# Weight-block sums of a Strassen up projection: made by transfers inside DRAM during attention, or by GpSimd during the MLP

## The chip, the cores and the metric

The kernel runs on one core of one Trainium2 chip. The metric is the device time of one execution in microseconds. A core has five engines that work beside one another: PE (TensorE, the matmuls; PEld are its weight loads), DVE (VectorE), ACT (ScalarE), POOL (GpSimd) and SP (SyncE, which only issues transfers here). Transfers are carried by 16 DMA engines of the core; SP, ACT and POOL can issue them.

## The reference

A two-layer encoder over two sequences (512 and 256 tokens, width 1024) that share the weights. Layer 0 mixes 2-D neighbourhood attention and grouped-query attention (GQA), layer 1 is differential attention. After each attention comes a squared-ReLU MLP of width 4096:

```python
for layer in range(DEPTH):
    ...                                   # attention of the layer, residual add
    h = rmsnorm(x, ln_mlp[layer])
    x = x + jnp.square(jax.nn.relu(h @ w_up[layer])) @ w_down[layer]
return rmsnorm(x, ln_f)
```

All arrays are float32.

## The kernel before

**Staging.** All 768 tokens are held together. The program is four stages in a row: `even_attention` (layer 0), `mlp(0)`, `odd_attention` (layer 1), `mlp(1)`. Activations and weights are split into a high and a low part (`wsplit`, L80 on ACT for the high part, L81 on DVE for the low part), and every product is three matmuls (high-high, high-low, low-high).

**The up projection.** `h @ w_up` is done by Strassen's method in Winograd's form: seven products in place of eight, on 2 x 2 blocks. The columns of `w_up` are walked in 16 steps (`mp`, 0 to 15) of 256 columns; each step has four weight blocks a11, a22, a12, a21 of 128 x 512 values. Steps 0 and 1 use the plain blocks with eight products (while the sums of activations are made by `second()`), steps 2 to 15 use the seven products, 84 matmuls each. The seven need four sums of weight blocks, s1 = a21 + a22, s2 = s1 + a11, s3 = a11 + a21, s4 = a12 + s2 (signs are in the layout). Products are called by number: 1 needs a11, 2 a12, 3 s4, 4 a22, 5 s1, 6 s2, 7 s3. PE runs them in the order 1, 3, 2, 6, 4, 7, 5. In `weights()` the blocks are loaded by two transfers of 512 KB into `wraw` tiles (3 buffers), POOL makes the four sums (L843) into `s` tiles, and the splits are written in the order (1,4), (6,5), (7,3), (2). High and low parts have 4 buffers each (`whilo`).

**The norm in it.** The MLP's RMSNorm is applied late: `nm.rstd()` (L161 to L166) sums squares by matmul, `ms` is made by DVE (L164) and the power -1/2, `rt`, by POOL (L166); `nm.spread` (L178, `pb`) spreads it over partitions by PE. This happens while steps 2 and 3 run. `finish(z)` writes the squared activations to DRAM tiles `T`, from ACT's queue (L879) and POOL's (L887), and the down projection reads them back (`tr`).

**The attentions.** `attention(units, chain, targets)` weaves 48 attention units (softmax of one token tile of one head or pair) into a chain of projection steps; `targets` says up to which step of the chain each unit comes. Weights of the projections are loaded by SP, group by group, through the same 3 `wraw` buffers (`wload`, L74). POOL does small things there: the powers `rn` of the q/k norms (L356, L357), the scaling of one GQA softmax map (L502), parts of the rotary embedding (L677, L678) and the powers of layer 1's sub-norm (L724).

**What sets the order.** The order of the instructions on an engine is not that of the text. A planner takes the program as written and places instructions one by one, each as soon as its engine, its data and its buffers are free by the planner's own estimates of the costs; among those that are ready the one written earlier goes first. On the chip each engine then keeps that order strictly, and an instruction that waits holds up all that stand behind it on its engine.

Of the kernel before, what the change touches and what calls it, by code (L numbers as in the profile page):

```python
# [37 lines left out]
def kernel(ctx: ExitStack, tc: tile.TileContext, a: dict, y: bass.AP):  # L38
# [37 lines left out]
    def wsplit(hi, lo, raw, dve=False):  # L76
        if dve:
            nc.vector.tensor_copy(hi, raw)
        else:
            nc.scalar.activation(hi, raw, AF.Copy)  # L80
        nc.vector.tensor_tensor(out=lo, in0=raw, in1=hi.bitcast(F32), op=ALU.subtract)  # L81
# [151 lines left out]
                fn()  # L233
            self.due = []

    def attention(units, chain, targets):

        live = []
        n = len(targets) - 1
        for i in range(n):  # L240
            a, b = targets[i], targets[i + 1]
            chain.pull(a)
            live.append(units[i]())
            live[-1][0]()
# [56 lines left out]
    def even_attention():  # L301
# [306 lines left out]
                       lambda: out_proj("w_out_e", o, lambda m: a["xT"][:, m, :], x, 0)])  # L608
        units = [G(gqa_unit, j, t) for j in range(4) for t in range(TT)]
        units += [G(na_unit, p, t) for p in range(4) for t in range(TT)]  # L610
        attention(units, chain, ramp((52, 72, 88, 104, 120, 140, 172, 196, 232)))
        chain.drain()
        return o, x, es

# [1 line left out]
    def odd_attention(xs, nm, sg, spill):  # L616
# [121 lines left out]
            order += [G(proj_v, h // 2)] * (h % 2 == 0) + [G(proj_qk, h)]  # L738
        chain = Chain(order + [lambda: out_proj("w_out_o", o, lambda m: spill[:, m, :], x, 0)])
        units = [G(diff_unit, h, t) for h in range(8) for t in range(TT)]  # L740
        attention(units, chain, ramp((56, 92, 128, 164, 200, 236, 272, 306, 336)))
        chain.drain()
        return o, x, es

# [24 lines left out]
    def mlp(layer, src, o, x, es):  # L769
# [47 lines left out]
        g2 = g2s.enter_context(tc.tile_pool(name="g2", bufs=4, side="right", reuse_waits="tile"))  # L817
        up = g2s.enter_context(tc.tile_pool(name="up", bufs=3, side="right", reuse_waits="tile"))

        def weights(plain=False):  # L820


            raws = []
            for _ in range(2):
                raw, loads = wload("w_up", 1024)
                loads[0]()
                raws.append(raw)
            a11, a22, a12, a21 = (r[:, i * 512 : (i + 1) * 512] for r in raws for i in range(2))
            if plain:
                out = {}  # L830
                for t, ij in zip(raws, (((0, 0), (1, 1)), ((0, 1), (1, 0)))):
                    hi, lo = whilo(1024)
                    wsplit(hi, lo, t)
# [5 lines left out]
            out = {}  # L839
            for ps_, t in (((1, 4), raws[0]), ((6, 5), sa), ((7, 3), sb), ((2,), raws[1])):  # L840
                if t is sa:
                    for d_, x_, y_ in ((s1, a21, a22), (s2, s1, a11), (s3, a11, a21), (s4, a12, s2)):
                        nc.gpsimd.tensor_tensor(out=d_, in0=x_, in1=y_, op=ALU.add)  # L843
# [49 lines left out]
        ws = [weights(True) for _ in range(2)]  # L893
        for w in ws:
            z = ztile()
            pss = [bank(n) for n in (1, 6, 2, 4)]
# [17 lines left out]
            return th  # L914

        for mp in range(2, FF // 256):
            w = weights()
# [322 lines left out]
```

## Time and profile before

| what | value |
|---|---|
| time, median of 3 runs | 1790.25 us (1785.74 to 1792.01) |
| the profiled execution | 1793.21 us, span 1791.2 us, mean granted TensorE clock 0.982 |
| PE, PEld busy | 96%, 92% of the span |
| DVE, ACT, POOL busy | 77%, 46%, 33% |
| moved by transfers | 235.42 MB, mean 131 GB/s |
| layer 0's attention units on PE | 59.7 to 349.6 us |
| layer 0's up products | about 372 to 634 us |
| layer 1's attention units on PE | 924 to 1247 us |
| layer 1's up products | about 1272 to 1534 us |

How to read the rows. Times are microseconds from the start of the span; a mean of one instruction is in nanoseconds. A group's row is: line, engine, operation, out<-in, shapes, count | busy us, mean ns | idle time of the engine just before, and what ended most of it. In a table by stretches each engine has its busy time and the number of its instructions; the last three columns are the granted clock, the mean busy share of the 16 DMA engines and the GB/s. A row "A L1 <- B L2: x, n, y" says that A's instructions of L1 waited for B's of L2, x us in all, n times, y at most. In a timeline, the first two numbers are start and duration, and brackets hold the idle time before and what ended it; neighbours of one kind are merged. In the queues' rows stand packets, MB and the share of 16 engines' span that the packets took; an issue's row ends with KB each and the median time from issue to landing. q1 are SP's transfers, q10 ACT's, q0 POOL's. "SPq" and the like are an engine's issuing side.

### The profile page before, as it was taken

To read this page: it belongs to the slowest core of one execution; us is meant where nothing else is said; L and a number is where in the kernel's file an instruction comes from. 1 tells how busy PE (TensorE), PEld (TensorE's weight loads), DVE (VectorE), ACT (ScalarE), POOL (GpSimd) and SP (SyncE) were. 2 spreads that over 40 slices of the span, in tenths; PEclk is the share of its full clock that TensorE was granted. 3 is DMA by queue.
4 is the path that set the end of the run, shared out by engine and by line. 5 is a ranking of instruction groups with operands and counts; after the bars stand their busy time and mean duration, and the time that the engine had idled before them with its cause. 6 is when DMAs were issued, how large, how long until landed. Compare 5 with 4: busy or idle time off the path is not lost.

```text
span 1791.2 us, 28400 instructions
## 1 busy us (share of the span) xinstructions
PE 1728.0 (96%) x10994; PEld 1644.2 (92%) x10994; DVE 1385.5 (77%) x2182; ACT 827.2 (46%) x1509; POOL 583.7 (33%) x456
## 2 busy tenths in 40 slices
PE   7999999998999999999999999999988999999997
PEld 7887888898999989999999999988988999899997
DVE  7777746597888867799656767776878888787995
ACT  6665544363333444444435555554633334444441
POOL 2321000023555404475021212220225554053750
PEclk8999999999999999999999999999999999999998
DMA  5111223312554587664311101112125545977621
GB/s 173 41 33 37 68 71 104 121 48 72 189 163 164 182 329 294 245 204 158 97 46 48 48 25 45 54 57 95 48 69 180 166 166 170 337 271 258 223 89 71
DMA packets 74598, 235.42 MB, mean 131 GB/s; under 512 B 7904, under 2 KB 25056, under 8 KB 74464
## 3 DMA queue, kind: packets, MB, share of 16 engines
q1 hardware_dynamic: 52480, 186.93, 31.1%
q0 software_dynamic: 7168, 25.17, 3.8%
q10 hardware_dynamic: 14816, 21.52, 3.3%
q8 instruction: 86, 1.41, 0.3%
q14 instruction: 48, 0.39, 0.1%
HBM read 182.47 MB, written 50.33 MB: 130 GB/s over the span
## 4 chain that ended last, share of the span: by engine, by line
PE 79%; DVE 10%; issue 4%; ACT 3%; POOL 2%; DMA 2%; POOLq 0%; DVEq 0%; SPq 0%; ACTq 0%
PE dn L1019 26%; PE up L857 18%; PE dqk L190 8%; PE opa L202 5%; PE dvp L190 4%; PE opb L202 2%; PE npa L202 2%; PE ds L268 2%; PE dpv L716 2%; DVE t L792 2%; DVE wlo L81 1%; PE qp L190 1%; PE vp L190 1%; PE npv L596 1%; PE npb L202 1%
## 5 line engine op out<-in xcount | busy, mean ns | idle before, releaser
L857 PE MATMUL up<-c,whi 128*128 128x384 f32 x1824 | 472.8, 341 | 3.0 <-DVE z L865 3.0
L1019 PE MATMUL dn<-th,whi 128*128 128x384 f32 x1792 | 464.6, 340 | 8.4 <-DVE th L117 5.7
L857 PEld LDWEIGHTS up<-c,whi 128*128 128x128 f32 x1824 | 335.6, 191 | 3.7 <-issue 3.6
L1019 PEld LDWEIGHTS dn<-th,whi 128*128 128x128 f32 x1792 | 328.4, 189 | 9.7 <-DVE th L117 6.3
L857 PE MATMUL up<-c,wlo 128*128 128x384 f32 x912 | 311.0, 342 | 13.3 <-DVE wlo L81 13.1
L1019 PE MATMUL dn<-th,wlo 128*128 128x384 f32 x896 | 304.4, 340 | 0.0
L985 POOL TENSOR_TENSOR ch<-ch,wd 128x1024 f32<-128x1024 f32 x60 | 190.7, 3189 | 127.6 <-DVE wlo L81 97.4
L843 POOL TENSOR_TENSOR s<-wraw 128x512 f32<-128x512 f32 x56 | 91.7, 1652 | 368.8 <-DMA wraw<-in_w_up_dram 284.9
L81 DVE TENSOR_TENSOR wlo<-ch,whi 128x1024 fp32r<-128x1024 f32 x88 | 165.7, 1894 | 36.6 <-ACT whi L80 35.1
L857 PEld LDWEIGHTS up<-c,wlo 128*128 128x128 f32 x912 | 173.9, 191 | 15.4 <-DVE wlo L81 15.4
L80 ACT ACTIVATE whi<-ch 128x1024 fp32r<-128x1024 f32 x88 | 93.4, 1064 | 184.7 <-PE dn L1019 147.1
L1019 PEld LDWEIGHTS dn<-th,wlo 128*128 128x128 f32 x896 | 169.7, 189 | 0.0
L81 DVE TENSOR_TENSOR wlo<-wraw,whi 128x1024 fp32r<-128x1024 f32 (+3 forms) x132 | 146.7, 1114 | 27.5 <-ACT whi L80 27.1
L80 ACT ACTIVATE whi<-wraw 128x1024 fp32r<-128x1024 f32 (+3 forms) x128 | 117.0, 916 | 91.6 <-PE up L857 42.7
L117 DVE TENSOR_TENSOR th<-tr,th 128x1536 fp32r<-128x1536 f32 x56 | 131.3, 2347 | 7.6 <-ACT th L116 7.0
L190 PE MATMUL dqk<-whi,xh 128*128 128x256 f32 x384 | 115.9, 302 | 3.1 <-ACT dv L646 3.1
L190 PE MATMUL dqk<-whi,xl 128*128 128x256 f32 x384 | 108.5, 283 | 0.0
L190 PE MATMUL dqk<-wlo,xh 128*128 128x256 f32 x384 | 108.3, 282 | 0.0
L701 ACT ACTIVATE de<-ds,m 128x512 f32<-128x512 f32 (+1 forms) x96 | 58.3, 612 | 81.7 <-DVE m L699 81.7
L878 ACT ACTIVATE z<-z 128x1536 f32<-128x1536 f32 x32 | 47.7, 1490 | 103.0 <-DVE z L876 103.0
L865 DVE TENSOR_TENSOR z<-up,z 128x384 f32<-128x384 f32 x168 | 92.4, 551 | 2.6 <-issue 1.3
L80 ACT ACTIVATE whi<-s 128x1024 fp32r<-128x1024 f32 x56 | 59.5, 1064 | 67.0 <-PE up L857 67.0
(217 smaller groups left out, 3784.4 us busy)
## 6 DMA issues: line engine op xcount, KB each, us to landing
wd<-in_w_down_dram SPq DMA_DIRECT2D x84, 512.0 KB, 4.1
tr<-T SPq DMA_DIRECT2D x56, 768.0 KB, 5.4
wraw<-in_w_up_dram SPq DMA_DIRECT2D x64, 512.0 KB, 3.6
T<-t POOLq DMA_DIRECT2D x64, 384.0 KB, 3.1
T<-z ACTq DMA_DIRECT2D x32, 576.0 KB, 3.0
ch<-in_w_down_dram SPq DMA_DIRECT2D x28, 512.0 KB, 6.0
wraw<-in_w_in_o_dram SPq DMA_DIRECT2D x24, 512.0 KB, 3.6
wraw<-in_w_in_e_dram SPq DMA_DIRECT2D x16, 512.0 KB, 3.6
```

The costliest lines, as they stand in the source:

```text
L80: nc.scalar.activation(hi, raw, AF.Copy)
L81: nc.vector.tensor_tensor(out=lo, in0=raw, in1=hi.bitcast(F32), op=ALU.subtract)
L117: nc.vector.tensor_tensor(out=lo, in0=src, in1=hi.bitcast(F32), op=ALU.subtract)
L190: nc.tensor.matmul(ps[:, :256], st[:, tk], col(k, part, 0, 256), start=(k == 0 and i == 0), stop=(k == KD - 1 and i == 2))
L202: nc.tensor.matmul(ps[:, : e - s], w, mv[:, s:e], start=(k == 0 and i == 0), stop=(k == nk - 1 and i == 2))
L701: nc.scalar.activation(e, s, AF.Exp, bias=m, scale=1.0, accum_out=l2[:, c : c + 1])
L843: nc.gpsimd.tensor_tensor(out=d_, in0=x_, in1=y_, op=ALU.add)
L857: nc.tensor.matmul(ps, part[a_][:, base + k * P : base + (k + 1) * P], t[:, b_], start=start and k + i == 0, stop=stop and k == 3 and i == 2)
L865: nc.vector.tensor_tensor(out=out, in0=x_, in1=y_, op=op)
L878: nc.scalar.activation(z, z, AF.Square)
L985: nc.gpsimd.tensor_tensor(out=t, in0=t, in1=new.pop((i, rp)), op=ALU.add)
L1019: nc.tensor.matmul(ps, w[a_][:, c : c + P], th[:, b_, q], start=i + q + k == 0, stop=i == NG - 1 and q == ND - 1 and k == 2)
```

## The change

The four sums of steps 2 to 15 are no longer made by POOL in the MLP. New DRAM tiles `S{layer}_{mp}`, one for each chunk of `CH = 2` steps, receive them during the attention ahead. `up_sums(layer)` returns, for each of the 7 chunks, four stages: `copies` issues four transfers on SP that copy blocks from `w_up` into the tile; then POOL issues two accumulating transfers (they add another block of `w_up` onto a copied one), and two more that add one part of the tile onto another. Each of these eight transfers moves 2 steps x 128 rows x 512 values (512 KB, rows of 2 KB). `order` interleaves the stages of neighbouring chunks, and `attention` takes them from the list `side` while it writes its units, from unit 3 on. In the MLP, `weights(mp)` loads the sums from the DRAM tile (two transfers of 512 KB) and the blocks that are used plain (three transfers of 256 KB), and the splits are written in the order (1,4), (7,3), (2), (6,5). POOL's additions of L843 are gone.

```diff
+    CH = 2
+    wsums = {}
+
+    def up_block(layer, mp, n, pair, half):
+        v = a["w_up"].rearrange("(l m a p h c) -> l m a p h c", l=2, a=2, p=P, h=2, c=512)
+        return v[layer, mp : mp + n, pair, :, half]
+
+    def up_sums(layer):
+        out = []
+        for mp in range(2, FF // 256, CH):
+            t = dram.tile([2, CH, P, 2, 512], F32, name=f"S{layer}_{mp}")
+            for i in range(CH):
+                wsums[layer, mp + i] = t[:, i]
+            blk = lambda pair, half, mp=mp: up_block(layer, mp, CH, pair, half)
+
+            def copies(t=t, blk=blk):
+                for j, half in ((0, 1), (1, 0)):
+                    for pair in range(2):
+                        nc.sync.dma_start(t[j, :, :, pair], blk(pair, half))
+
+            acc = lambda d, s_: nc.gpsimd.dma_start(d, s_, accum_op=ALU.add)
+            out.append((copies, lambda t=t, blk=blk: (acc(t[1, :, :, 0], blk(1, 1)), acc(t[0, :, :, 1], blk(0, 1))),
+                        lambda t=t: acc(t[0, :, :, 0], t[1, :, :, 0]), lambda t=t: acc(t[1, :, :, 1], t[0, :, :, 0])))
+        n = len(out)
+        order = []
+        for i in range(n + 3):
+            for j in range(4):
+                if 0 <= i - j < n:
+                    order.append(out[i - j][j])
+        return order
+
-    def attention(units, chain, targets):
+    def attention(units, chain, targets, side=()):
+        side, n_side = list(side), len(side)
         live = []
         n = len(targets) - 1
         for i in range(n):
             a, b = targets[i], targets[i + 1]
+            while side and n_side - len(side) < n_side * (i - 2) / (n - 6):
+                side.pop(0)()
             chain.pull(a)
...
-        attention(units, chain, ramp((52, 72, 88, 104, 120, 140, 172, 196, 232)))
+        attention(units, chain, ramp((52, 72, 88, 104, 120, 140, 172, 196, 232)), up_sums(0))
...
-        attention(units, chain, ramp((56, 92, 128, 164, 200, 236, 272, 306, 336)))
+        attention(units, chain, ramp((56, 92, 128, 164, 200, 236, 272, 306, 336)), up_sums(1))
...
-        def weights(plain=False):
-            raws = []
-            for _ in range(2):
-                raw, loads = wload("w_up", 1024)
-                loads[0]()
-                raws.append(raw)
+        def weights(mp, plain=False):
...
-            sa, sb = (up.tile([P, 1024], F32, tag="s", name="s", bufs=3) for _ in range(2))
-            s2, s1, s3, s4 = (r[:, i * 512 : (i + 1) * 512] for r in (sa, sb) for i in range(2))
-            out = {}
-            for ps_, t in (((1, 4), raws[0]), ((6, 5), sa), ((7, 3), sb), ((2,), raws[1])):
-                if t is sa:
-                    for d_, x_, y_ in ((s1, a21, a22), (s2, s1, a11), (s3, a11, a21), (s4, a12, s2)):
-                        nc.gpsimd.tensor_tensor(out=d_, in0=x_, in1=y_, op=ALU.add)
+            s_ = wsums[layer, mp]
+            for ps_ in ((1, 4), (7, 3), (2,), (6, 5)):
                 w = 512 * len(ps_)
+                if 6 in ps_ or 7 in ps_:
+                    t = up.tile([P, 1024], F32, tag="s", name="s", bufs=3)
+                    nc.sync.dma_start(t.rearrange("p (h c) -> p h c", h=2), s_[7 in ps_])
+                else:
+                    t = wpool.tile([P, 1024], F32, tag="wraw", name="wraw", bufs=3)[:, :w]
+                    for half in range(len(ps_)):
+                        nc.sync.dma_start(t[:, half * 512 : half * 512 + 512], up_block(layer, mp, 1, 2 in ps_, half)[0])
                 hi, lo = whilo(w)
-                wsplit(hi, lo, t[:, :w])
+                wsplit(hi, lo, t)
                 for i, p in enumerate(ps_):
                     out[p] = (hi, lo), i * 512
             return out
```

More of the change, by code (lines that the diff above doesn't have):

```diff
@@ L818, in mlp @@
         up = g2s.enter_context(tc.tile_pool(name="up", bufs=3, side="right", reuse_waits="tile"))
-        def weights(plain=False):
-            raws = []
-            for _ in range(2):
-                raw, loads = wload("w_up", 1024)
-                loads[0]()
-                raws.append(raw)
-            a11, a22, a12, a21 = (r[:, i * 512 : (i + 1) * 512] for r in raws for i in range(2))
+        def weights(mp, plain=False):
+            out = {}
             if plain:
-                out = {}
-                for t, ij in zip(raws, (((0, 0), (1, 1)), ((0, 1), (1, 0)))):
+                for pair, ij in enumerate((((0, 0), (1, 1)), ((0, 1), (1, 0)))):
+                    raw = wpool.tile([P, 1024], F32, tag="wraw", name="wraw", bufs=3)
+                    for half in range(2):
+                        nc.sync.dma_start(raw[:, half * 512 : half * 512 + 512], up_block(layer, mp, 1, pair, half)[0])
                     hi, lo = whilo(1024)
-                    wsplit(hi, lo, t)
+                    wsplit(hi, lo, raw)
                     for i, b in enumerate(ij):
@@ L836, in weights @@
                 return out
-            sa, sb = (up.tile([P, 1024], F32, tag="s", name="s", bufs=3) for _ in range(2))
-            s2, s1, s3, s4 = (r[:, i * 512 : (i + 1) * 512] for r in (sa, sb) for i in range(2))
-            out = {}
-            for ps_, t in (((1, 4), raws[0]), ((6, 5), sa), ((7, 3), sb), ((2,), raws[1])):
-                if t is sa:
-                    for d_, x_, y_ in ((s1, a21, a22), (s2, s1, a11), (s3, a11, a21), (s4, a12, s2)):
-                        nc.gpsimd.tensor_tensor(out=d_, in0=x_, in1=y_, op=ALU.add)
-                w = 512 * len(ps_)
+            s_ = wsums[layer, mp]
+            for ps_ in ((1, 4), (7, 3), (2,), (6, 5)):
+                w = 512 * len(ps_)
+                if 6 in ps_ or 7 in ps_:
[5 more added lines that the diff above has]
+                        nc.sync.dma_start(t[:, half * 512 : half * 512 + 512], up_block(layer, mp, 1, 2 in ps_, half)[0])
                 hi, lo = whilo(w)
-                wsplit(hi, lo, t[:, :w])
+                wsplit(hi, lo, t)
                 for i, p in enumerate(ps_):
@@ L890, in ztile @@
             return up.tile([P, 4, HT], F32, tag="z", name="z", bufs=3).rearrange("p (i n) t -> p i (n t)", n=2)
-        ws = [weights(True) for _ in range(2)]
+        ws = [weights(mp, True) for mp in range(2)]
         for w in ws:
@@ L916, in mlp @@
         for mp in range(2, FF // 256):
-            w = weights()
+            w = weights(mp)
             one = lambda n: product(bank(n), w[n], n)
```

## The prediction

> **What bounds the kernel now.** I read the page first (engine shares, queues, issues), then the up stage (windows, PE's waits, the timeline at its start), then the queues that issue transfers.
>
> ```profile
> span 1791.2 us, 28400 instructions
> PE 1728.0 (96%) x10994; PEld 1644.2 (92%) x10994; DVE 1385.5 (77%) x2182; ACT 827.2 (46%) x1509; POOL 583.7 (33%) x456
> ...
> q1 hardware_dynamic: 52480, 186.93, 31.1%
> ...
> q10 hardware_dynamic: 14816, 21.52, 3.3%
> ```
>
> TensorE is busy 96% of the span, so nothing that only frees another engine can bring much; what can be won is PE's idle time in the up stage. Stage by stage (PE, PEld, DVE, ACT, POOL, each with its instruction count; clock, DMA share, GB/s):
>
> ```profile
> 420.00:460.00 40.00, 34.22 (x190) 33.35 (x190) 28.22 (x37) 12.76 (x13) 13.71 (x12) 0.94 0.42 146
> 460.00:610.00 150.00, 150.00 (x860) 150.00 (x860) 132.81 (x152) 58.45 (x61) 90.22 (x63) 1.00 0.49 166
> ```
>
> In the steady part of layer 0's up stage PE has no idle time (150.00 of 150) while POOL makes its sums beside it. PE waits only at the start, where the first two Strassen blocks (mp 2 and 3) run. Its waits in 365 to 640 us, then in 1262 to 1540 us (total, times, longest), and the timeline around one of them:
>
> ```profile
> PE up L857 <- DVE wlo L81: 5.5, 2, 3.8
> PE pb L178 <- POOL rt L166: 2.3, 1, 2.3
> ...
> PE up L857 <- DVE wlo L81: 7.7, 3, 3.8
> PE pb L178 <- POOL rt L166: 2.3, 1, 2.3
> ...
> 432.14 0.16 DVE L164 TENSOR_SCALAR ms<-ss 128x6 f32<-128x6 f32 x1
> 433.55 1.71 POOL L843 TENSOR_TENSOR s<-wraw,s 128x512 f32<-128x512 f32 x1
> 435.23 1.32 POOL L166 TENSOR_TENSOR rt<-ms,nhalf 128x6 f32<-128x6 f32 x1
> 436.60 1.60 PE L178 MATMUL pb<-ident,rt 128*128 128x128 f32 x12 [2.28 <-POOL rt L166]
> ```
>
> The norm's `ms` was ready at 432.30, but `rt` stood behind a weight sum on POOL until 435.23, and PE lost 2.28 us for it.
>
> **The change, part by part.**
>
> *1. The additions go.* 112 POOL additions:
>
> ```profile
> L843 POOL TENSOR_TENSOR s<-wraw 128x512 f32<-128x512 f32 x56 | 91.7, 1652 | 368.8 <-DMA wraw<-in_w_up_dram 284.9 <-DVE wlo L81 44.5 <-ACT whi L80 17.9
> L843 POOL TENSOR_TENSOR s<-s,wraw 128x512 f32<-128x512 f32 x28 | 67.5, 2411 | 0.3
> L843 POOL TENSOR_TENSOR s<-wraw,s 128x512 f32<-128x512 f32 x28 | 41.4, 1480 | 1.9
> ```
>
> are 200.6 us of POOL, of which PE felt 2 x 2.3 = 4.6 us (rt). That goes whole: 435.23 - 432.30 = 2.93 us earlier covers 2.28.
>
> ```profile
> L81 DVE TENSOR_TENSOR wlo<-s,whi 128x1024 fp32r<-128x1024 f32 x56 | 69.3, 1237 | 4.7 <-ACT whi L80 4.7
> L857 PE MATMUL up<-c,whi 128*128 128x384 f32 x1824 | 472.8, 341 | 3.0 <-DVE z L865 3.0
> ```
>
> *2. The splits' order* becomes (1,4), (7,3), (2), (6,5), the order in which the products use them. Of the 5.5 + 7.7 = 13.2 us that PE waits for `wlo`, I count one split of 1.24 us in each layer that no longer stands ahead of the second product's weights, 2.5 us; ends 0 and 13.2, since DVE, at 132.81 of 150, is late next. Parts 1 and 2: -7 us, ends -4.6 and -17.8.
>
> *3. Loads in the MLP.* Each of the 28 Strassen blocks now loads 1.75 MB by 5 issues in place of 1 MB by 2. In a block of 84 matmuls of 341 ns (28.6 us) that adds 27 GB/s to 166 at a DMA share of 0.49: hidden by that free half; 84 more issues of 0.33 us go to an SP that mostly waits. Cost 0; without the cover 0.75 MB at 166 GB/s, 4.7 us a block.
>
> *4. 56 copies on SP and 56 accumulating transfers on POOL* (7 chunks of two blocks in each layer, 4 and 4 each, every one 512 KB). POOL's issues cost at most what it pays today (L887 below, 0.73 us): 41 us on an engine with 67% idle, 0 on the path. The transfers themselves carry the forecast. First, where they run:
>
> ```profile
> L1103 ACTq DMA_DIRECT2D sg<-in_subln_dram x1: 453/453/453, 1.7 to 1.7; - x1
> L887 POOL DMA_DIRECT2D T<-t x64 | 46.7, 730 | 115.1 <-DVE t L865 114.9
> 0.74 0.41 ACTq L57 DMA_DIRECT2D gains<-in_gains_dram  x1
> ...
> 1.67 0.45 ACTq L1103 DMA_DIRECT2D sg<-in_subln_dram  x1
> 0.75 0.39 SPq L315 DMA_DIRECT2D x<-in_xT_dram  x1
> ...
> 2.60 0.43 SPq L315 DMA_DIRECT2D x<-in_xT_dram  x1
> 4.62 0.33 SPq L74 DMA_DIRECT2D wraw<-in_w_in_e_dram  x1
> SPq L74 <- DMA gains<-in_gains_dram: 1.6, 1, 1.6
> ...
> 11.74 9.13 SPq L74 DMA_DIRECT2D wraw<-in_w_in_e_dram  x3
> 36.32 7.45 SPq L74 DMA_DIRECT2D wraw<-in_w_in_e_dram  x4
> SPq L74 <- DVE wlo L81: 25.4, 5, 15.3
> ```
>
> The load of `sg` is written behind the whole first MLP, yet it issues at 1.7 us: the planner puts forward whatever has nothing to wait for. A copy reads an input and writes a DRAM tile of its own, so all 56, of both layers, are free from the start, and SP stands idle from 20.9 to 36.3 us waiting for a weight slot. So I expect them in the first 200 us, not spread over the two attentions. The accumulating ones follow on POOL, each waiting there for its copies; behind them in POOL's order stand `rn` and the GQA scaling, for which ACT, DVE and then PE wait. And the queue is finite: five loads by SP (0.75 to 2.60 us) and three by ACT (0.74 to 1.67) were out when SP stopped, until `gains` had landed. With eight copies out, every weight load waits for copies.
>
> Then, how long one takes:
>
> ```profile
> wraw<-in_w_up_dram SPq DMA_DIRECT2D x64, 512.0 KB, 3.6
> wraw<-in_w_out_e_dram SPq DMA_DIRECT2D x8, 384.0 KB, 3.0
> nv<-nv SPq DMA_DIRECT2D x8, 96.0 KB, 2.1
> ```
>
> Every transfer shown has 128 or 64 partitions outermost. The copies begin with a count of two (the chunk's two blocks, not contiguous in `w_up`), then 128 rows of 2 KB. Two ends: all 16 engines, or one for each of the two, 256 KB per engine. No row decides; I take two engines, reading the outermost count as what a transfer is shared out by, and put 8 in 10 on it as a judgement. The Trainium skill's page "DMA: Bandwidth & Descriptors", section "Why a DMA increments its semaphore by 16 and not by 1", says that the number of engines is the largest up to 16 that divides the slowest dimension of both patterns, and on the SP queue the lowest-numbered ones. By that rule every copy runs on the same two engines; the trace neither shows nor denies it.
>
> The rate of one engine: q1 moved 186.93 MB in 31.1% of 16 x 1791.2 us, 21 GB/s; q10 likewise 23. Those have SBUF at one end. Upper end 22; lower end 11, if reading and writing DRAM share one path. Between them stands the landing of loads: 128 KB more, 8 KB an engine, take 0.6 us more (3.0 to 3.6), 13.7 GB/s. I take that, as the one between the ends: 262,144 B / 13.7 GB/s = 19.1 us a copy; ends 11.9 and 23.8. The same page, section "Latency and other measured facts", gives 214 GB/s for copies between DRAM tensors over all engines, an estimate of 13.4 GB/s each; by it the 56 would take 1096 us and the sum be 24 us more.
>
> Since all use the same two engines, they follow one another: 56 x 19.1 = 1070 us (667 to 1333). Every weight load needs its share of those engines too, and stands behind them in one queue, so PE cannot run ahead. What lies beside other work is the part of the attention that the planner sets among the copies: 56 x 0.43 us of issue (24 us) to 56 x 3.6 us (202 us); middle, 113. The accumulating transfers: 0 if other engines carry them, 56 x 32 KB / 13.7 = 134 us if they spread evenly over all and delay the two; I take 0, they have a queue of their own and run beside the copies.
>
> **Sum**, against the profiled 1793.2 us (span 1791.2 and 2.0 around it; 3 us, 0.2%, over the median 1790.25): 1793 + 1070 - 113 - 7 = 2743; from the median, **2740 us**. Ends: 1790 + 667 - 202 - 18 = 2237; 1790 + 1333 + 134 - 24 - 5 = 3228.
>
> **Rivals.** *A: two engines, but in the place where they are written* (from unit 3 to unit 30 of each attention's 48).
>
> ```profile
> L268 PE MATMUL gs<-gk,gq x144: 271/392/792, 59.7 to 191.0; 64*128 64x512 f32 x96, 64*128 64x256 f32 x48
> L268 PE MATMUL ns<-n,n x144: 271/279/384, 196.4 to 349.6; 64*128 64x256 f32 x144
> L268 PE MATMUL ds<-d,d x192: 273/387/398, 924.1 to 1246.6; 64*128 64x512 f32 x128, 64*128 64x256 f32 x64
> ```
>
> Layer 1's units last 323 us; 27 of 48 are about 181 us, against 28 x 19.1 = 535 us of copies: +354. Layer 0's last 290 us, 27 of 48 some 163: +372. 2510 us; with 11.9 us a copy (333 us a layer) 2100. For it: the weight loads issue no earlier than their slots allow, close to their use. Against it: they wait for slots, and `sg`, which waits for none, went to the front.
>
> *B: 16 engines, at the front.* 512 KB over 16 engines at 13.7 GB/s is 2.4 us; eight out are 19 us ahead of any load. The loads that matter:
>
> ```profile
> 40.96 1.04 ACT L80 ACTIVATE whi<-wraw 128x1024 fp32r<-128x1024 f32 x1
> 55.63 1.05 ACT L80 ACTIVATE whi<-wraw 128x1024 fp32r<-128x1024 f32 x1
> ```
>
> The load issued at 36.32 lands 3.6 us later, 1 us before its split: 18 us lost there. Accumulating transfers at the same price on the same engines: up to as much again. 1790 + 36 - 7 = 1819.
>
> *C: other side, faster.* The transfers spread over 16 engines and in attention time with slack: 29.4 MB of copies at 219 GB/s are 134 us of engines that are 11% and 16% busy there.
>
> ```profile
> 60.00:196.00 136.00, 128.12 (x889) 107.90 (x888) 106.84 (x230) 84.40 (x228) 33.56 (x38) 0.97 0.11 36
> 924.00:1247.00 323.00, 322.31 (x2538) 292.20 (x2537) 227.47 (x605) 171.20 (x488) 71.02 (x128) 1.00 0.16 50
> ```
>
> 1790 - 7 = 1783. It decides as soon as a copy lands within the slack of the loads behind it: some 10 us for eight. Against it: the outermost two, and `sg`.
>
> **Numbers.** My forecast 0.70 (own range 2240 to 3230), A 0.10, B 0.12, C 0.08. Forecast and A alone fill about 0.75 of their own ranges, so the range reaches down into B: 1810 to 3230. This kernel's measurement can tell about 0.3% (5 us) from no change. Faster by more: most of C, 0.05; within: the rest of C and a little of B, 0.04; slower: 0.91.
>
> **What would show it.** Right: copies of 512 KB that take over 100 us from issue to landing with eight out, SP and POOL waiting for them, PE idle in long stretches of the first 1100 us, the rest of the kernel as before, and a low DMA share (two of 16 engines, about 0.13) in that time. Right for the gain: no `pb` wait for `rt`. Wrong: copies landing in under 10 us (16 engines), or issued in the attentions' units instead of in the first hundreds of us (A). What would make it wrong most of all is the count of engines, then the rate of one engine between two places in DRAM.

## The result and the profile after

The changed kernel takes 2126.5 us (median of 4 runs, 2122.5 to 2140.9), the kernel before 1790.0 us (4 runs): ratio 1.190, interval 1.184 to 1.196, +336 us where +950 was forecast. The profiled execution's span is 2127.4 us.

The page of the changed kernel, engines, queues and one issue row:

```profile
span 2127.4 us, 28553 instructions
PE 1800.9 (85%) x10994; PEld 1688.2 (79%) x10994; DVE 1318.0 (62%) x2182; ACT 828.0 (39%) x1509; POOL 454.9 (21%) x400
...
q1 hardware_dynamic: 80176, 238.32, 32.2%
q0 software_dynamic: 72576, 54.94, 13.2%
...
S<-in_w_up_dram POOLq DMA_DIRECT2D x28, 512.0 KB, 32.5
```

POOL is down from 583.7 to 454.9 us of work, and PE from 96% to 85% of a longer span. Stretches of the changed kernel, the neighbourhood units of layer 0 (the `ns` scores) and the units of layer 1, with columns as in the prediction:

```profile
243.00:570.00 327.00, 191.26 (x1157) 161.29 (x1157) 100.97 (x262) 71.08 (x176) 43.55 (x31) 0.78 0.59 136
1224.00:1597.00 373.00, 329.92 (x2542) 296.07 (x2541) 229.01 (x606) 170.95 (x488) 79.56 (x136) 0.95 0.24 63
```

The neighbourhood units had lasted 154 us (196 to 350) and now last 327; layer 1's units 373 instead of 323. Layer 0's 24 GQA units, 57 to 191 us, stand where they stood, although the first copies run beside them. Read from the first and last matmuls of each stage, layer 0's attention lost 228 us, the first MLP 72, layer 1's attention some 50; the last MLP gained 14.

The copies on SP (L259) and the bias loads of the neighbourhood units (L606) in the timeline of SP's queue, changed kernel:

```profile
38.28 56.53 SPq L259 DMA_DIRECT2D S<-in_w_up_dram  x7
...
105.93 73.98 SPq L259 DMA_DIRECT2D S<-in_w_up_dram  x8
...
348.14 0.67 SPq L259 DMA_DIRECT2D S<-in_w_up_dram  x1
348.92 11.46 SPq L606 DMA_DIRECT2D nbias<-in_bias_dram  x1
...
361.14 25.53 SPq L606 DMA_DIRECT2D nbias<-in_bias_dram  x1
```

SP is held inside its issues, and later a bias load behind one copy is held 11 to 26 us. The issues of the copies that start in the first 210 us, then all of them (duration min/median/max in ns, then first and last start), and the moved bytes and the busy times from 110 to 180 us:

```profile
L259 SPq DMA_DIRECT2D S<-in_w_up_dram x16: 628/10122/12282, 13.0 to 169.8; - x16
...
L259 SPq DMA_DIRECT2D S<-in_w_up_dram x56: 611/700/16296, 13.0 to 1301.9; - x56
...
DMA packets 1737, 3.63 MB, mean 52 GB/s; under 512 B 18, under 2 KB 18, under 8 KB 1732
110.00:180.00 70.00, 54.57 (x277) 39.71 (x277) 52.27 (x107) 40.11 (x105) 15.40 (x17) 0.79 0.13 52
```

While the queue is full a copy takes 10.1 us (median), and all 16 engines together move 52 GB/s. Their mean busy share is then 0.13 (two of 16 are 0.125), and PE still works 54.57 of the 70 us. The last copy starts at 1302 us: they did not all go to the front. The waits up to 620 us that answer to it:

```profile
POOL S L261 <- DMA S<-in_w_up_dram: 306.4, 9, 48.7
ACT ne L623 <- DVE m L621: 121.3, 20, 39.8
DVE ne L621 <- DMA nbias<-in_bias_dram: 105.8, 9, 38.3
PE npt_ps L319 <- DVE ne L628: 104.1, 14, 34.9
```

Bias to DVE to PE: this chain says that slow copies delay bias loads. It is a true wait of this run, but, as the last pair of experiments shows, not the whole cause.

### The profile page after: what moved, and what is told of

Same layout as the page of the kernel before. It is cut to its first block, busy times and chain, and to the rows that moved or that the text cites. A ratio compares the mean times of both kernels' runs of the same rounds, so it can differ in the third digit from the quotient of the medians.

```text
span 2127.4 us, 28553 instructions
## 1 busy us (share of the span) xinstructions
PE 1800.9 (85%) x10994; PEld 1688.2 (79%) x10994; DVE 1318.0 (62%) x2182; ACT 828.0 (39%) x1509; POOL 454.9 (21%) x400
## 3 DMA queue, kind: packets, MB, share of 16 engines
q0 software_dynamic: 72576, 54.94, 13.2%
## 5 line engine op out<-in xcount | busy, mean ns | idle before, releaser
L1059 PE MATMUL dn<-th,whi 128*128 128x384 f32 x1792 | 475.2, 346 | 34.8 <-ACT whi L80 13.8
L1059 PEld LDWEIGHTS dn<-th,whi 128*128 128x128 f32 x1792 | 334.6, 193 | 39.2 <-ACT whi L80 14.6
L897 PE MATMUL up<-c,wlo 128*128 128x384 f32 x912 | 311.6, 342 | 11.9 <-DVE wlo L81 11.9
L1059 PE MATMUL dn<-th,wlo 128*128 128x384 f32 x896 | 308.8, 345 | 7.6 <-DVE wlo L81 7.6
L81 DVE TENSOR_TENSOR wlo<-wraw,whi 128x1024 fp32r<-128x1024 f32 (+3 forms) x132 | 134.9, 1026 | 108.3 <-ACT whi L80 107.7
L81 DVE TENSOR_TENSOR wlo<-ch,whi 128x1024 fp32r<-128x1024 f32 x88 | 159.0, 1823 | 64.7 <-ACT whi L80 64.5
L117 DVE TENSOR_TENSOR th<-tr,th 128x1536 fp32r<-128x1536 f32 x56 | 126.0, 2255 | 45.1 <-ACT th L116 44.4
L927 POOL DMA_DIRECT2D T<-t x64 | 46.5, 727 | 384.9 <-DVE t L905 360.7
L261 POOL DMA_DIRECT2D S<-S x28 | 25.6, 916 | 447.0 <-DMA S<-in_w_up_dram 363.7
L116 ACT ACTIVATE th<-tr 128x1536 fp32r<-128x1536 f32 x56 | 82.5, 1478 | 68.0 <-DMA tr<-T 51.3
L319 PE MATMUL npt_ps<-ident,ne 128*128 128x128 f32 x96 | 19.4, 327 | 104.2 <-DVE ne L628 104.1
## 6 DMA issues: line engine op xcount, KB each, us to landing
S<-in_w_up_dram POOLq DMA_DIRECT2D x28, 512.0 KB, 32.5
```

Source lines behind the costliest of these rows:

```text
L116: nc.scalar.activation(hi, src, AF.Copy)
L117: nc.vector.tensor_tensor(out=lo, in0=src, in1=hi.bitcast(F32), op=ALU.subtract)
L319: nc.tensor.transpose(out=pt[:, i * P : (i + 1) * P], in_=b, identity=ident)
L897: nc.tensor.matmul(ps, part[a_][:, base + k * P : base + (k + 1) * P], t[:, b_], start=start and k + i == 0, stop=stop and k == 3 and i == 2)
L927: nc.gpsimd.dma_start(T[i][:, j : j + 2, q], t)
L1059: nc.tensor.matmul(ps, w[a_][:, c : c + P], th[:, b_, q], start=i + q + k == 0, stop=i == NG - 1 and q == ND - 1 and k == 2)
```

## The experiments

All times stand against the kernel before at 1787 to 1790 us on the same chip. Kernels without an interval ran once. A comparison of the compiled programs serves too: the share of PE's instructions in an attention that stand more than 16 places from where they stood before, written "order moved", layer 0 / layer 1.

**The MLP by itself.** First without copies and accumulating transfers:

```diff
-   nc.sync.dma_start(t.rearrange(...), s_[7 in ps_])        # the sums from DRAM
+   # blocks of w_up in their place; up_sums() issues nothing
```

> No copies and no accumulating transfers; the MLP loads the same bytes from w_up in place of the sums, so the sums are left out. What is left is the change in the MLP alone: no POOL additions, five loads a step, the new order of splits. Theory 1: 1790 less 7 to 18 us by the prediction's parts 1 to 3; by the undisturbed second MLP of the changed kernel, where out projection and up stage took 271.1 us in place of 284.8, twice 13.7, so about 1763 us. A rival, that this second MLP gained because its attention came late and left prefetched loads: 1783 us or more.

1769.9 us, ratio 0.990 (0.988 to 0.991): 18.5 us gained. The same with the old order of the splits:

```diff
-            for ps_ in ((1, 4), (7, 3), (2,), (6, 5)):
+            for ps_ in ((1, 4), (6, 5), (7, 3), (2,)):
```

> No copies, no accumulating transfers and no additions: the MLP loads blocks of w_up in place of the sums (the sums are left out), with the splits in the order of the kernel before, (1,4), (6,5), (7,3), (2). Theory (two parts: the additions' rt wait of 2 x 2.3 us, and the order, of which the run with the order alone gained 12 us): the additions by themselves are worth 5 to 8 us, 1781 to 1785 us. Rival (the late POOL sums delayed the splits; without them the old order costs nothing): 1768 to 1774 us, as with the new order.

1771.8 us, ratio 0.992 (0.990 to 0.994): the rival was right, the order is hardly needed when POOL makes no sums. The opposite, the kernel before with the new order alone:

```diff
-            for ps_, t in (((1, 4), raws[0]), ((6, 5), sa), ((7, 3), sb), ((2,), raws[1])):
+            for ps_, t in (((1, 4), raws[0]), ((7, 3), sb), ((2,), raws[1]), ((6, 5), sa)):
```

> The kernel before with the splits alone in the order (1,4), (7,3), (2), (6,5), POOL's additions kept. If the order of the splits carries the MLP's gain: 1763 to 1780 us. If the absent additions carry it: 1788 to 1792 us, and PE still waits 2.3 us for rt in each layer.

1776.7 us, ratio 0.993 (0.992 to 0.995). It keeps every sum and is the fastest of the kernels that compute the whole result, ahead of the kernel before and of the changed one. The two parts overlap: 16 and 12 us alone, 18.5 together. The first 88 us of layer 0's up stage, before, then without copies, then the order alone:

```profile
372.00:460.00 88.00, 78.42 (x430) 76.70 (x429) 73.05 (x98) 39.59 (x61) 27.42 (x20) 0.94 0.26 89
```

```profile
372.00:460.00 88.00, 85.19 (x485) 83.98 (x484) 71.57 (x108) 43.39 (x65) 7.34 (x9) 0.98 0.39 131
```

```profile
372.00:460.00 88.00, 82.43 (x459) 80.59 (x458) 77.85 (x99) 41.48 (x63) 34.59 (x23) 0.96 0.29 96
```

PE does 55 matmuls more in the same 88 us (x430 to x485) while its busy time grows by only 6.8 us: the granted clock went from 0.94 to 0.98. PE's waits over the whole span, before and then without copies:

```profile
PE up L857 <- DVE wlo L81: 13.1, 5, 3.8
PE pb L178 <- POOL rt L166: 5.8, 3, 2.3
```

```profile
PE up L897 <- DVE wlo L81: 2.0, 2, 1.0
...
PE pb L178 <- POOL rt L166: 1.2, 1, 1.2
```

15.7 us of waits go, 18.5 us are gained (the other 2.8 us are not explained by these rows); the kernel without copies and with the old order has 3.4 us of waits for `wlo`.

**Copies and accumulating transfers, by engines.** Written with the 128 rows first, the same 512 KB go another way:

```diff
-  nc.sync.dma_start(t[j, :, :, pair], blk(pair, half))
+  nc.sync.dma_start(t[j, :, :, pair].rearrange("m p c -> p m c"), blk(pair, half).rearrange("m p c -> p m c"))
-  acc = lambda d, s_: nc.gpsimd.dma_start(d, s_, accum_op=ALU.add)
+  acc = lambda d, s_: nc.gpsimd.dma_start(d.rearrange("m p c -> p m c"), s_.rearrange("m p c -> p m c"), accum_op=ALU.add)
```

Both edits, then the copies alone, then the accumulating ones alone, then the changed kernel without its accumulating transfers (`acc = lambda d, s_: None`), then both edits to the copies and that:

> The same eight transfers of each chunk with the 128 rows written ahead of the two steps in the pattern, so the same bytes and rows. Theory 1 (a transfer is shared out by its outermost count, here two): copies now spread over all engines, SP no longer spends 10 us in each, accumulating transfers from w_up land in about the 9 us of those within S instead of 32.5 us; the time falls to 1770 to 1800 us. Theory 2 (the volume in DRAM and the waiting of POOL for dependent transfers cost it, whatever the engines): over 2000 us, with copies still holding SP. In between, 1800 to 2000 us, both have a part.

> Only the copies get the rows outermost; the accumulating transfers keep the two. If SP's copies are the larger part: the copies go to the front and fill all engines as with all on rows (1919 us), and POOL's slow accumulating ones hold rn and the GQA scaling behind them: 1930 to 2050 us. If the accumulating ones are harmless once the copies are quick: under 1920 us.

> Only the accumulating transfers get the rows outermost; the copies keep the two. Theory 1, with SP held by copies as the larger part and POOL's slow accumulating ones as the smaller: near the kernel that has only the copies (2025 us), 2010 to 2060 us, POOL's waits for transfers from w_up well under the changed kernel's 375 us. Rival (what the accumulating ones cost is their dependence and order, not their engines): 2100 to 2140 us.

> The changed kernel's copies as they are (outermost count two) without the accumulating transfers, so the sums are left out. Theory 1 with SP as the place of the loss: the copies that hold SP some 10 us each in layer 0 (about 210 us in all) still delay the weight loads, so 1950 to 2050 us, and layer 0's attention still ends over 150 us late. Rival (POOL's waits for accumulating transfers are the loss): 1780 to 1850 us.

> As the all-engine run (rows outermost, all copies at the front), but the accumulating transfers are left out, so the sums in DRAM are not complete. Theory by volume: 29.4 MB instead of 59 MB stand ahead, so the +148 us of layer 0 falls to about half, and POOL waits for no copy: 1815 to 1860 us. Rival (POOL's waits carry it, the copies by themselves are hidden): 1770 to 1790 us, as without any copies. Rival (the copies alone carry it, eight out ahead of every weight load): 1895 us or more.

| copies | no accumulating | accumulating, rows first | accumulating, two first |
|---|---|---|---|
| none | 1769.9 | | |
| rows first | 1770.5 | 1919.5 (ratio 1.072, 1.070 to 1.074) | 2013.0 |
| two first (as changed) | 2025.3 | 2098.4 | 2126.5 |

Both edits together (1919.5) fell between their two theories. Copies with rows first cost nothing (1770.5 against 1769.9), though all 56 are issued by 133 us and the DMA share of the first 150 us is 0.88. That missed its theory by volume, and ended at the first rival's 1770 to 1790. Copies with two first cost 255 us by themselves. The accumulating transfers as changed, two first, cost 101 us on top of these, and 243 on top of quick copies; with rows first they cost 73 and 149. Rows first on the accumulating ones alone, 2098.4, missed 2010 to 2060 and came just under the rival's 2100 to 2140. Order moved: with rows first in both 0 / 0, with two first .52 / .10 (no accumulating), .52 / .22 (as changed), and .44 / .46 where only the copies have rows first.

**How a count is shared out.** Eleven chained transfers of 512 KB behind the finished kernel, each waiting for the last, first dimension 2, 2, 4, 8, 16, 128 on SP, then 2, 4, 8, 16, 128 accumulating on POOL:

```diff
+    for n in (2, 2, 4, 8, 16, 128):
+        nc.sync.dma_start(rows(big.rearrange("p f -> (p f)"), n), rows(a["w_up"], n))
+    for n in (2, 4, 8, 16, 128):
+        nc.gpsimd.dma_start(rows(big.rearrange("p f -> (p f)"), n), rows(a["w_up"], n), accum_op=ALU.add)
```

> The kernel before, and behind its end eleven transfers of 512 KB (256 rows of 2 KB from w_up into DRAM), each waiting for the one before, that differ only in the outermost count of their patterns: copies by SP with 2, 2, 4, 8, 16, 128, then accumulating ones by POOL with 2, 4, 8, 16, 128. Theory 1 (shared out by the outermost count): copies land in 12, 12, 7, 5, 4, 4 us, by 256 KB per engine in the 10.2 us by which SP was held in each, and the accumulating ones in 25 to 30 us at 2, halving with each doubling to 16, then equal. Rival (all 16 engines serve each of them, and the changed kernel's slow transfers come from crowding): all copies land within 20% of one another, and so do the accumulating ones.

The issues on SP and then on POOL (brackets: idle before, ended by the transfer ahead):

```profile
1788.32 0.77 SPq L1117 DMA_DIRECT2D big<-in_w_up_dram  x1
...
1801.56 0.62 SPq L1117 DMA_DIRECT2D big<-in_w_up_dram  x1
...
1814.11 0.62 SPq L1117 DMA_DIRECT2D big<-in_w_up_dram  x1
...
1836.45 1.99 POOL L1119 DMA_DIRECT2D big<-in_w_up_dram  x1 [57.44 <-DMA big<-in_w_up_dram]
1860.84 1.39 POOL L1119 DMA_DIRECT2D big<-in_w_up_dram  x1 [22.40 <-DMA big<-in_w_up_dram]
1874.95 1.08 POOL L1119 DMA_DIRECT2D big<-in_w_up_dram  x1 [12.72 <-DMA big<-in_w_up_dram]
1884.21 0.89 POOL L1119 DMA_DIRECT2D big<-in_w_up_dram  x1 [8.17 <-DMA big<-in_w_up_dram]
1890.70 1.14 POOL L1119 DMA_DIRECT2D big<-in_w_up_dram  x1 [5.60 <-DMA big<-in_w_up_dram]
```

A copy with a count of two takes 13.2 and 12.6 us alone, one with four 8.2. Accumulating, the steps are 24.4 (two), 14.1, 9.3 and 6.5 us (16). They fall with the count but do not halve. An estimate from the first two steps is a fixed 3.8 us and 41.2 us shared by the count; it gives 9.0 and 6.4 for the others. So the first dimension sets the engines, as the prediction read it, and with two first accumulating costs about twice a copy.

**Other chunk sizes.**

```diff
-    CH = 2
+    CH = 7
```

> Chunks of 7 steps in place of 2: the outermost count is 7, a transfer moves 1.75 MB, and there are 2 chunks a layer, 8 + 8 transfers in place of 28 + 28. Theory 1: 7 engines serve each, 256 KB per engine as before, so SP is held about 10 us for each of 8 copies a layer (some 80 us in place of 280) and the time falls to 1830 to 1950 us. Rival (one transfer's cost follows its bytes): SP is held 35 us for each and the time stays over 2050 us.

1937.3 us: accumulating transfers of 1792 KB land in 44.1 us against 32.5 for 512 KB; both are 256 KB per engine when shared by the first dimension. The time is in the theory's range. Order moved .49 / 0, and layer 1's units took 322.6 us, as before.

```diff
-    CH = 2
+    CH = 1
```

> CH = 1: a transfer moves one step's block, 256 KB, and the 128 rows are the first dimension of its pattern; 112 copies and 112 accumulating transfers instead of 56 and 56, the sums complete. Theory (the outermost count shares a transfer out over the engines): landing of a copy and of an accumulating transfer falls below 15 us, SP is not held for 10 us in an issue, all copies are issued by 350 us, and the time is near the all-engine run, 1890 to 1960 us. Rival (what held the transfers was their size or the rows of 2 KB, not the count of two): 2050 us or more.

2088.3 us. The theory was right about the transfers: copies land in 6.1 us, accumulating ones in 6.2, and no issue takes over 2.2 us. It was wrong about their place (the last copy is issued at 1361 us, not by 350) and about the time, which is the rival's 2050 or more, though not for the rival's reason. Order moved .41 / .61. This was the run that pointed away from slow transfers.

**Why accumulating costs with all engines.** Against the kernel with rows first everywhere (1919.5 us, order not moved, and the whole loss in layer 0's GQA units). Its POOL timeline:

```profile
104.89 1.17 POOL L261 DMA_DIRECT2D S<-S  x1 [8.85 <-DMA S<-in_w_up_dram]
105.65 1.49 POOL L397 TENSOR_TENSOR rn<-ss,nhalf 128x4 f32<-128x4 f32 x1
...
107.37 1.03 POOL L543 TENSOR_TENSOR ge<-ge,ri 128x512 f32<-128x512 f32 x1
111.45 1.22 POOL L261 DMA_DIRECT2D S<-S  x1 [3.04 <-DMA S<-S]
```

and its waits up to 340 us:

```profile
POOL S L261 <- DMA S<-in_w_up_dram: 129.4, 17, 20.3
ACT work L413 <- POOL rn L398: 97.6, 14, 18.4
...
PE gpt_ps L484 <- POOL ge L543: 54.6, 7, 14.2
POOL S L261 <- DMA S<-S: 52.3, 10, 8.8
```

`rn` and the scaling `ge` stand in POOL's order behind issues that wait for a landing. Three runs vary this: layer 1's sums in tiles named as layer 0's; accumulating onto the first eight pieces in turn, so that nothing fresh is waited for; and 16 of the 128 rows only.

```diff
-            t = dram.tile([2, CH, P, 2, 512], F32, name=f"S{layer}_{mp}")
+            t = dram.tile([2, CH, P, 2, 512], F32, tag=f"S_{mp}", name=f"S_{mp}")
```

> Copies and accumulating transfers with rows outermost, as in the all-engine run, but layer 1's sums are written into layer 0's DRAM tiles, so layer 1's 28 copies cannot be issued before MLP 0 has read them. Theory (the all-engine run lost its +148 us because 59 MB of both layers stood ahead of layer 0's weight loads): half the volume at the front, so about half the loss: layer 0's attention ends 60 to 100 us earlier than there (ns ends 400 to 440 us instead of 497), the time is 1830 to 1870 us, layer 1's copies cost little. Rival (the loss is POOL's waits for the first copies, or a fixed delay of the first units, not the volume): layer 0 ends as late as there, ns at 480 us or more, 1900 us or more.

1916.8 us (ratio 1.072): the tiles were not shared after all, the last copy is issued at 246 us as without the edit, so it repeats the run and tells nothing on volume.

```diff
+                d = ring[len(turn) % 8][0]
+                nc.gpsimd.dma_start(d.rearrange("m p c -> p m c"), blk(1, 1).rearrange("m p c -> p m c"), accum_op=ALU.add)
```

> As the all-engine run (rows outermost), with all 112 transfers at their size, but the accumulating transfers add blocks of w_up in turn onto the first eight copied pieces, so that none waits for a copy just issued or for the transfer just before it (the sums come out as something else). Theory (POOL stands in its order waiting for each fresh copy, and the powers rn and the scaling ge behind it come late): POOL's wait for S falls from 180 us below 60, layer 0 ends near its old place (ns end 350 to 400 us), 1770 to 1825 us. Rival (the volume, 59 MB on engines that are over 90% busy for 300 us): 1890 us or more, ns end 470 us or more.

```diff
+  nc.gpsimd.dma_start(d[:, :16].rearrange("m p c -> p m c"), s_[:, :16].rearrange("m p c -> p m c"), accum_op=ALU.add)
```

> As the all-engine run, but each accumulating transfer adds only 16 of the 128 rows (64 KB instead of 512 KB), so the sums are mostly left out; the waits of POOL, copy by copy, stay, the volume falls from 59 to 33 MB. Theory (POOL's waits in its order): the waits get shorter with the less loaded engines but remain, one landing of some 3 to 6 us each: layer 0's ns ends at 390 to 460 us, 1810 to 1885 us. Rival (volume): as without accumulating transfers, ns end 350 us, 1770 to 1785 us.

1843.5 and 1788.3 us. Layer 0's attention is 47 and 17 us longer than before, against 148. The first fell between theory and rival: POOL still waited 137 us for landings, which took 15.1 us (median). The second lies below what I expected, near the volume rival. POOL's waits for `S` (182 us in the kernel with rows first everywhere, then 137 and 62) and the loss (148, 47, 17) fall together. With the smaller volume the landings got shorter too (median 6.2 us), so these runs do not separate the waits from the volume.

**Is it SP that is held?** Copies with two first, no accumulating transfers (2025 us), but issued by POOL; and again by SP, with the bias loads on ACT:

```diff
-                        nc.sync.dma_start(t[j, :, :, pair], blk(pair, half))
+                        nc.gpsimd.dma_start(t[j, :, :, pair], blk(pair, half))
```

> Copies with a count of two outermost as in the changed kernel, accumulating transfers left out (the sums are not complete), and the copies issued by POOL instead of SP. Theory (the 2025 us of these copies on SP come from SP being held about 10 us in an issue, with bias and weight loads queued behind): SP is never held, most of the loss goes, 1770 to 1860 us unless POOL is held in the same way, which its idle time before rn and ge would show. Rival (the two engines carry a share of every load, whoever issues the copies): 1980 us or more.

```diff
-                nc.sync.dma_start(b, a["bias"][p, BI[t]])
+                nc.scalar.dma_start(b, a["bias"][p, BI[t]])
```

> As the run with two-engine copies on SP and without accumulating transfers (2025 us; the sums are not complete), but the 24 or so bias loads of layer 0's neighbourhood units are issued by ACT instead of SP. Theory (each bias load is held about 10 us behind a copy in SP's queue, which paces those units): the ns units, 272 us long there, shrink to 160 to 210 us, the time falls by 60 to 120 us to 1905 to 1965 us; layer 1 stays slow. Rival (the bias loads wait on the two engines themselves, whatever the queue): ns as long as before, 2000 us or more.

1937.2 and 2099.9 us. Bias issues with copies on SP, then with copies on POOL:

```profile
L606 SPq DMA_DIRECT2D nbias<-in_bias_dram x20: 383/4113/10612, 284.8 to 500.4; - x20
```

```profile
L606 SPq DMA_DIRECT2D nbias<-in_bias_dram x20: 328/380/1351, 259.6 to 404.8; - x20
```

With POOL issuing, the median issue is 380 ns again and the neighbourhood units take 152 us as before; but GQA's now take 166 and layer 1's 359. It lies between both theories. The second is inconclusive: a weight load on SP waited 89.8 us for a bias load that ACT issued late, so a new wait hid the answer. Order moved .44 / .46 and .65 / .10: neither run had kept the order.

**The order alone.** 112 copies of 256 KB (CH = 1, no accumulating transfers). Both kernels issue the same transfers; only the dimension written first differs:

```diff
-                        nc.sync.dma_start(t[j, :, :, pair], blk(pair, half))
+                        nc.sync.dma_start(t[j, :, :, pair].rearrange("m p c -> p m c"), blk(pair, half).rearrange("m p c -> p m c"))
```

> CH = 1, 112 copies of 256 KB that land in about 6 us, the block's count of one written first, accumulating transfers left out (the sums are not complete). In this kernel 41% of PE's instructions of layer 0's attention and 31% of layer 1's stand more than 16 places from where they stood before. Theory (the order, laid out for slow copies, costs by itself): 1890 to 2020 us, ns units spread over 200 us or more, although no copy is slow and SP is not held. Rival (only slow transfers and waits for them cost): 1765 to 1785 us, as with quick copies from the front.

> As the run beside it, the same 112 copies of 256 KB and no accumulating transfers (the sums are not complete), but the 128 rows are written first; PE's order in the attentions is then that of the kernel before. Theory: 1765 to 1785 us, ns units 153 us long. Rival (112 issues or their volume cost by themselves): the same time as the run beside it.

2076.0 us with the block's count first, 1770.4 with rows first. Issues (KB, landing) and neighbourhood units of the first:

```profile
S<-in_w_up_dram SPq DMA_DIRECT2D x112, 256.0 KB, 5.3
...
237.00:476.00 239.00, 197.21 (x1149) 167.54 (x1149) 99.03 (x262) 71.16 (x176) 0.00 (x0) 0.85 0.29 95
```

and of the second:

```profile
S<-in_w_up_dram SPq DMA_DIRECT2D x112, 256.0 KB, 6.1
...
194.00:348.00 154.00, 153.13 (x1062) 134.12 (x1061) 88.26 (x252) 65.48 (x169) 0.00 (x0) 1.00 0.30 97
```

The landings are equally quick (the slow kernel's even quicker), yet 306 us lie between them. What differs is the order. PE's timeline in the neighbourhood units of the kernel before:

```profile
196.45 0.62 PE L268 MATMUL ns<-n,n 64*128 64x256 f32 x6
197.00 0.50 PE L202 MATMUL npa<-xh,whi 128*128 128x512 f32 x1
...
201.10 0.28 PE L202 MATMUL npb<-xh,wlo 128*128 128x256 f32 x1
201.22 0.60 PE L278 MATMUL npt_ps<-ident,ne 128*128 128x128 f32 x4
201.75 0.63 PE L268 MATMUL ns<-n,n 64*128 64x256 f32 x6
```

and of the slow one of the pair:

```profile
293.26 1.12 PE L319 MATMUL npt_ps<-ident,ne 128*128 128x128 f32 x4 [2.87 <-DVE ne L628]
294.30 1.01 PE L309 MATMUL ns<-n,n 64*128 64x256 f32 x6
295.24 2.07 PE L637 MATMUL npv<-npt,nv 128*128 128x128 f32 x8
300.18 1.12 PE L319 MATMUL npt_ps<-ident,ne 128*128 128x128 f32 x4 [2.87 <-DVE ne L628]
```

Before, 4.2 us of other matmuls, projections (`npa`, `npb`) and values of GQA among them, stand between a unit's scores and the next transposes, so the softmax of DVE and ACT is covered. In the slow kernel scores, transposes and values follow one another with nothing between: PE waits 2.87 us for `ne`, twice in these 10 us, and its matmuls are slower (ns x6 1.01 us instead of 0.62, clock 0.85). The projections run elsewhere in blocks: none starts between 270 and 320 us. No copy is involved in these waits: from 190 to 498 and from 1039 to 1567 us, which hold the rest of both attentions, ACT waits 1.4 us for landings in all, PE and DVE not at all.

Of the 306 us, 124 lie in layer 0's attention, 131 in layer 1's and 51 in the first MLP. In the attentions the order moved. In the MLP PE keeps it (0.3% moved) and waits 26 us for ACT, which it never does there in the quick kernel; the runs do not show why.

Kernels with the same order of PE show both sides. The changed kernel without accumulating transfers and the one with these rows first share PE's order in both attentions and the first MLP, yet lie 73 us apart: those are not PE's order. On the other hand, CH = 1 loses 122 us in layer 0's attention with and without accumulating transfers, in the same order. And layer 1's units last 359 us both with copies on POOL and with rows first on the copies alone, again in the same order.

## Why the prediction was wrong, point by point

- *1 and 2, the gain* was a term mis-sized: -7 with ends -4.6 and -17.8; the runs show -18.5. The wait for `rt` went as worked out, 4.6 us of it. Of the 13 us for `wlo` 2.5 were counted, and 10 to 11 went: these waits were late sums, and without POOL's sums they fell in either order. The other 2.8 us are not explained; in the 88 us shown the granted clock rose from 0.94 to 0.98.
- *3, five loads a block*: right. 1770 us with them all.
- *4, where they run.* "All 56 in the first 200 us" is what quick copies do (issued 13 to 133 us). The slow ones went one by one up to 1302 us. In the last pair the dimension written first alone moves the last of 112 copies from 136 to 1380 us, so the planner's places follow it.
- *4, two engines*: right, by the chain above and the DMA share of 0.13, which the prediction named as a sign. The Trainium skill's page "DMA: Bandwidth & Descriptors", section "Why a DMA increments its semaphore by 16 and not by 1", states a sharing by the slowest dimension; the steps of 24.4, 14.1, 9.3 and 6.5 us agree.
- *4, the rate*: 13.7 GB/s an engine was taken, 19.1 us a copy. In a stream a copy takes 10.1 us, 26 GB/s on each of two engines; alone 12.6 to 13.2 us, some 20. My lower end of 11.9 us was nearest. My upper end of 22 came from averages over whole queues, and an average over issues with gaps is no upper end. The Trainium skill's page "DMA: Bandwidth & Descriptors", section "Latency and other measured facts", has 214 GB/s for copies of 128 rows of 16 KiB between HBM tensors. Over 16 engines that would be 13.4 each by an estimate; the 52 GB/s that two engines moved here are twice that, and decide.
- *4, "all serial in the path"* is the step that failed. 56 x 10.1 would be 566 us even at the measured price, and the copies alone cost 255: at least 311 us of them, not 113, lay beside other work, as PE's 54.57 busy us of 70 with a full queue show. In the pair with quick copies no engine of the attentions waits for a copy, and the loss is 306. The forecast treated PE's order as given, and priced transfers; what moved was the order. The sign came out right, partly for another reason than the one given.
- *4, accumulating transfers at 0*: measured +101 on top of slow copies, +243 on top of quick ones (149 with rows first). I had named `rn` and the GQA scaling as standing behind them on POOL, and then counted only engines. Of the 101, 67 us lie in layer 0's attention, where PE's order is the same without them, and 42 in the first MLP; the share of POOL's 306 us of waits wasn't separated. The issues from `w_up` took POOL 2.2 us (median) and those within `S` 0.9, not 0.73.
- *Rival A* had the place in kind, spread over the kernel, and its lower number, 2100, is near 2126.5. That is luck: it has copies that follow one another and outlast the units beside them, 310 us in all, and nothing for the accumulating transfers.
- *Rival B* had the place (front, all engines, 1819) but priced a queue ahead of loads; such copies cost 0 and the accumulating ones all of it, 1919.5. *Rival C* failed by these alone: without them 1770 us.

Sum as measured: 1790 - 20 (with this pair's kernels, 1769.9) + 255 + 101 = 2126. **Open**: how the 255 splits between the order and copies that really hold SP. Waits for loads in the kernel with these copies alone:

```profile
DVE ne L621 <- DMA nbias<-in_bias_dram: 42.0, 5, 27.7
ACT whi L80 <- DMA wraw<-in_w_in_e_dram: 17.2, 2, 16.9
```

The slow kernel of the last pair has 0.2 us of these from 190 us on, so by an estimate some 59 of the 255 us are direct waits for loads; what follows from such waits is not in it. Copies that are slow on the chip in the order of before were not tried: what is written two first also changes the order. That an order laid out by the planner can cost as much without slow copies is shown: 124 and 131 us in the two attentions of the pair.

## What to carry to other kernels

Where a planner fixes the order of instructions, a new transfer has two costs: what it does on the chip, and how the planner reorders the rest around it. Look first at whether the engine that bounds the kernel runs its instructions in the same order as before, and write a transfer between DRAM tensors with its 128 rows first. An instruction that waits for a landing should not stand on an engine that softmax needs. And before moving work off an engine, try the order of what is left: here that alone gave 12 us at no cost.

## What had not been expected

- SP is held inside an issue, 10.1 us per copy with two first while its queue is full, where the same bytes with rows first took 0.6 us an issue; a bias load behind one copy was held up to 25.5 us.
- One accumulating transfer of 512 KB took 24.4 us with a first dimension of two, 6.5 us with 16.
- 29 MB of copies beside layer 0's GQA units, at a DMA share of 0.88, cost nothing that could be measured.
